# A hybrid encoder trunk on one core: the scan's first loads and first front move into the projections ahead of it, and filling products are left out in three places

## The chip, the core and the metric

One core of a Trainium2 chip. The metric is the device time of one execution in microseconds (us). Work runs on five engines with queues of their own: PE (TensorE, products; its weight loads are a row of their own, PEld), DVE (VectorE), ACT (ScalarE), POOL (GpSimd), and SP (SyncE), which here issues every DMA, in the order of its queue.

## The reference, cut to what matters

Two layers; each is a half-step FFN, a token mixer, a half-step FFN, with a layer norm after each. The first mixer is neighbourhood attention. The second, which is meant here, is a bidirectional RWKV-7 scan over 512 tokens, 16 heads of 64:

```python
xx = 0.5 * (x_prev + x_next) - x
xr, xw, xk, xv, xa, xg = (x + xx * mix[i] for i in range(6))
r, k, v = xr @ w_rkv[0], xk @ w_rkv[1], xv @ w_rkv[2]
wl = w0 + tanh(xw @ w1) @ w2                       # one per direction z
decay = exp(-exp(-softplus(-wl) - 0.5))
a = sigmoid(a0 + (xa @ a1) @ a2)
g = sigmoid(xg @ g1) @ g2
kk = normalised(k * k_k);  k_z = k * (1 + (a - 1) * k_a)
# per head, direction and token, with w, k_z, kk*a of that token:
sa = state @ (-kk)
state = state * w + outer(sa, kk * a) + outer(v, k_z);  y = state @ r
return (norm(y, forward + backward) + bonus(r, k_z, v)) * g @ w_out
```

## The kernel before, in words

Four FFNs, the attention and the scan follow each other. Weights are split by ACT and a second engine into a high and a low part, and a product is three products (`mm3`: lines 226, 227, 228).

**The projections** (`rwkv_project`) run in this order on PE, which keeps the order of the program text there: the keys (eight banks), the ranks `pw` and `pa`, the norm sums `ss` of the keys (L692), the receptances of the first pair of heads `pr` (L700; its inputs, the mixes `raws`, are computed by DVE at L648 into four `tmp` tiles in turn and stored as d_xr), the decays of direction 0 (`decays(0)`: 24 products, each evacuated by ACT and DVE and stored as d_lw), the gate's two ranks (L612), the decays of direction 1, and eight gate rows: six products each with the second gate weights `g2`, evacuated and stored as d_g. What the scan needs of all this it loads again from memory. Other engines and SP follow an order that a planner makes at build time from its own estimates: an instruction is placed when its inputs and its buffer are there, earlier text first.

**The scan** (`Scan`) treats pairs of heads, hp = 0 to 7. For each pair and direction `front` multiplies the decays with a triangle matrix (`tri`, L1234, cumulated decays), takes two exponentials, forms `a` (three products with `a2u` and `ah`) and builds the tiles `ar` and `bk`; `grams` (L1293) multiplies those; then come tails, values, an inversion on POOL, a chain over the chunks and the outputs. `load` fetches a pair's k, iv and a2. In the scan PE, ACT and DVE run in the order of lists (`SEQ`), one per slot n = -2 to 7. Ahead of slot -2, `run` loads ah, tri and the first pair, issues 33 filling products, and runs `front(0, 0)`; slot -2 begins with 17 more. Its list begins `g0 v f1 f1 f1 f1 f1 f1 g0 l g0 r r`: the first gram, the values' weights (`wv`), the second front, the next pair's `load`, and then `r`, steps of `receptances`. These are the receptances of pairs 1 to 7 (L1001, banks y and m); for them eight tiles of d_xr are loaded into az2, xs8 and xs9 and a weight of 512 KB at a time into other tiles of the scan, the first one after the eight.

A filling product (`busy`, L326) multiplies the identity by itself; nothing reads its result. It is there to keep PE at work while it would wait.

From slot 6 on, `outs` multiplies finished pairs with the output weights; the first five weights are loaded into the tiles wv, ar, ar, bk, bk.

The scan's tiles lie in two pools that open when the projections' pools have closed: `rwe` at the upper end of SBUF, over the weight pool, and `rwb` over everything else.

Of the kernel before, what the change touches and what calls it, by code (L numbers as in the profile page):

```python
# [10 lines left out]
F32 = mybir.dt.float32  # L11
# [79 lines left out]
def flat2(ap):  # L91
    return ap[:, :D], ap[:, D:]
# [6 lines left out]
class Trunk:  # L99
# [79 lines left out]
    def bank(self, tag="bank"):  # L179
        return self.ps.tile([P, 512], F32, name=tag, tag=tag, bufs=self.banks.get(tag))  # L180

# [397 lines left out]

    def rwkv_project(self, dram, xraw, w_rkv, w1, w2, a1, g1, g2, heads):  # L580

        nc = self.nc
        with self.pool("rwa") as pool:
            with self.behind(self.mid):
# [76 lines left out]
            with self.tc.manual_schedule(engines=MANUAL):  # L661
# [24 lines left out]
                low_rank(0, g1[:, :P], 5)  # L686
                g1b = pool.tile([P, ND, 32], F32, name="g1b")
# [9 lines left out]
                nc.sync.dma_start(dram["iv"], iv)  # L697
                pr = self.bank()
                for c, t in raws(0, dram["xr"]):
                    nc.tensor.matmul(pr, wr[:, c, :], t, start=c == 0, stop=c == ND - 1)  # L700
                with self.behind(self.lo, self.hi, self.mixed):
# [6 lines left out]
                def decays(z):  # L708
                    u = self.load_unit(w2[z])
                    for t in range(NT):  # L710
                        for h in range(2):
# [7 lines left out]
                            nc.sync.dma_start(dram["lw"][:, z, t, ws], th)  # L719
# [276 lines left out]
class Scan:  # L996
# [5 lines left out]

    def __init__(self, k, pool, dram, consts, a2, w_r, w_v, w_out):
        self.k, self.nc, self.pool, self.dram, self.a2, self.w_r, self.w_v, self.w_out = k, k.nc, pool, dram, a2, w_r, w_v, w_out
        nc = self.nc
        self.opened = ExitStack()
        early = self.early = self.opened.enter_context(k.pool("rwe", "right"))
        self.first = {}
        self.tri = early.tile([P, 2, P], F32, name="tri")
        self.mask = early.tile([P, 2, 2, CH], F32, name="mask")  # L1010
        self.onesb = early.tile([P, P], F32, name="onesb")
        self.eye = consts["eye"]
        self.ah = early.tile([P, 2, S], F32R, name="ah")
        self.xv = pool.tile([P, ND, S], F32, name="xv")
        self.consts = consts
# [12 lines left out]


        self.az = [(early if i == 2 else pool).tile([P, 2, NU, CH], F32, name=f"az{i}") for i in range(3)]  # L1030
        for i in range(2):
            self.clear(i)
        self.free = list(range(NBUF))
        self.taken, self.st, self.py = {}, {}, {}

# [3 lines left out]
    def tile(self, tag, shape, bufs=1, dtype=F32):  # L1039
        if tag in self.first:  # L1040
            return self.first.pop(tag)
        pool = self.early if tag in EARLY_TAGS else self.pool
        return pool.tile(shape, dtype, name=tag, tag=tag, bufs=bufs)
# [54 lines left out]
    def run(self, late, lead, ln):  # L1098
        with self.k.tc.manual_schedule(engines=MANUAL_SCAN):
            raw = self.tile("e", [P, S], 2)  # L1100
            for dst, src in ((raw, self.dram["ah"]), (self.tri, self.consts["tri"])):
                self.nc.sync.dma_start(dst, src)
            list(self.load(0))
            self.k.split(self.ah[:, 0, :], self.ah[:, 1, :], raw)
            self.k.busy(self.k.bank("c"), 33)
            list(self.front(0, 0))
            for n in ("mask", "onesb"):
                self.nc.sync.dma_start(getattr(self, n), self.consts[n])
            self.zs = []
# [12 lines left out]
            next(self.ending)  # L1122
# [59 lines left out]
    def slot(self, n):  # L1182
# [19 lines left out]
    def load(self, hp):  # L1202
# [11 lines left out]
        k.split(p.a2u[:, 0], p.a2u[:, 1], raw)  # L1214
        p.pc = tile_("pc", [P, NC, 2], 4)
        p.qd = tile_("qd", [P, NU, 32], 2)
        p.qc = tile_("qc", [P, NU, 32], 2)
        p.az = self.az[hp % 3]
        p.units, p.ar, p.bk = [], [], []
        yield  # L1220

    def front(self, hp, z):
# [7 lines left out]
        lw = tile_("lw", [P, NT, P], 2)  # L1230
        nc.sync.dma_start(lw, self.dram["lw"][:, z, :, hp * P : (hp + 1) * P])
        pi = k.bank("a")
# [11 lines left out]
        nc.scalar.activation(th, pa, AF.Tanh, scale=0.5, bias=k.col(C_A0H + z, hp))  # L1244
        ar = tile_("ar", [P, NC, 2, CH], 2)
        bk = tile_("bk", [P, NC, 2, CH], 2)
        at, rt = ar[:, way, 0, :], ar[:, way, 1, :]
# [14 lines left out]
        if z == 0:  # L1262
            nc.vector.scalar_tensor_tensor(p.iv, p.k, k.col(C_KKH, hp), p.iv, ALU.mult, ALU.mult)
        kz = tile_("kz", [P, S], 2)
        nc.scalar.activation(kz, th, AF.Identity, scale=k.col(C_KA1, hp), bias=k.col(C_KA2, hp))
# [219 lines left out]
    def outs(self):  # L1485
# [114 lines left out]
def trunk_kernel(tc, x, ffn_w_in, ffn_w_out, ln_g, ln_b, cols, w_qkv, b_qkv, bias, mask, w_o, b_o,  # L1600
                 w_rkv, w1, w2, a1, a2, g1, g2, rw_out, heads, tri, smask, onesb, eye, out):
    nc = tc.nc
    with ExitStack() as ctx:
# [12 lines left out]
        with k.activations(), k.psum(bank=8), k.weights(3):  # L1616
            k.load_x(grid(x))
            xT = k.new_xT()
            k.fill = {0: 11}
            for t in range(NT):  # L1620
# [8 lines left out]
            with ExitStack() as xs:  # L1629
                with k.behind(*k.last):  # L1630
                    xraw = k.ffn(xT, ffn_w_in[1, 0], ffn_w_out[1, 0], 3, lambda: XRaw(k, xs.enter_context(k.pool("xr"))))
                k.store_x(grid(dram["x"]))
                k.rwkv_project(dram, xraw.x, w_rkv, w1, w2, a1, g1, g2, heads)
        with ExitStack() as late:
            with k.pool("rwb") as pool:
                scan = Scan(k, pool, dram, dict(tri=tri, mask=smask, onesb=onesb, eye=eye), a2, w_rkv[0], w_rkv[2], rw_out)
# [79 lines left out]
```

## Time and profile before

| | |
|---|---|
| runs | 2238.38, 2242.78, 2242.82 us (median 2242.78) |
| the profiled execution | 2241.5 us, its span 2239.7 us |
| PE, DVE, ACT, POOL busy | 98%, 47%, 43%, 63% of the span |
| granted clock of PE, mean | 0.994 |
| DMA | 328.84 MB, mean 147 GB/s |
| filling products of the three places (L326, two passes each) | 22 passes from 1.37 us on; 66 from 1425.77 on; 34 from 1438.05 on |
| gate rows | 1411.5 to 1425.8 us |
| first receptance product of the scan | 1450.38 us |

How to read the profile: times are us from the start of the span. A row of the timeline has start, duration, engine, line, operation, the tiles out<-in, the count, and in brackets the engine's idle time before it with what ended it. In a window's row each engine has its busy time and, in brackets, its instructions; then come PE's granted clock (1.00 is full speed), the DMA engines' share, and GB/s. A row of the DMA issues has the tiles, the queue, the count, KB of each, and the median time from issue to landing. A busy PE is not a useful one: filling products count like all others.

### The profile page before, as it was taken

The numbers are of one execution on the slowest core, as the hardware profiler recorded it, in microseconds if no ns is written. First come the engines' busy times: TensorE is split into PE (matmuls) and PEld (weight loads), VectorE is DVE, ScalarE is ACT, GpSimd is POOL, SyncE is SP. The second block draws the span as 40 slices with busy tenths as digits, with TensorE's granted clock in tenths as the row PEclk, the third lists the DMA queues.
The fourth block names the chain that finished last, engine by engine and source line by source line (L and its number), as shares of the span: only waits on it lengthen the run. The fifth ranks groups of instructions, "written<-read, shape, count | busy, mean of one in ns | idle before, by whom it ended". The sixth has DMA issues, their size and how long they took to land. (4 is left out here: it accounts for less than half of the span.)

```text
span 2239.7 us, 35440 instructions
## 1 busy us (share of the span) xinstructions
PE 2187.5 (98%) x13972; PEld 1720.2 (77%) x13972; DVE 1063.5 (47%) x1524; ACT 957.6 (43%) x1678; POOL 1409.6 (63%) x1234
## 2 busy tenths in 40 slices
PE   8999999999999999999999999899999999999998
PEld 7888888887888888888888875535666657888886
DVE  2333356376433333643333587325788635333345
ACT  3333345377343333433333433336777633333333
POOL 6878855554487886588787442044776722888754
PEclk9999999999999999999999999999999999999999
DMA  6444463432344445454444545754454743544443
GB/s 199 143 143 147 145 230 97 131 93 84 110 141 144 145 143 170 135 184 141 142 137 140 197 131 191 231 158 126 114 141 111 207 151 99 160 142 136 141 169 122
DMA packets 350498, 328.84 MB, mean 147 GB/s; under 512 B 48458, under 2 KB 277450, under 8 KB 350332
## 3 DMA queue, kind: packets, MB, share of 16 engines
q1 hardware_dynamic: 350332, 326.58, 46.8%
q8 instruction: 110, 1.80, 0.3%
q14 instruction: 56, 0.46, 0.1%
HBM read 262.26 MB, written 47.74 MB: 138 GB/s over the span
## 5 line engine op out<-in xcount | busy, mean ns | idle before, releaser
L222 POOL TENSOR_TENSOR w<-raw,w 128x1024 fp32r<-128x1024 f32 x200 | 489.4, 2449 | 246.3 <-ACT w L221 222.7
L226 PE MATMUL bank<-xT,w 128*128 128x512 f32 x1408 | 549.3, 390 | 0.0
L227 PE MATMUL bank<-xT,w 128*128 128x512 f32 x1408 | 548.0, 389 | 0.0
L228 PE MATMUL bank<-xT,w 128*128 128x512 f32 x1408 | 547.9, 389 | 0.0
L221 ACT ACTIVATE w<-raw 128x1024 fp32r<-128x1024 f32 (+1 forms) x204 | 215.3, 1058 | 329.9 <-POOL ts L780 138.3
L428 DVE SCALAR_TENSOR_TENSOR ar<-bank,tmp 128x512 f32<-128x512 f32 x88 | 60.9, 692 | 578.3 <-PE bank L228 568.7
L228 PEld LDWEIGHTS bank<-xT,w 128*128 128x128 f32 x1408 | 264.3, 188 | 55.3
L227 PEld LDWEIGHTS bank<-xT,w 128*128 128x128 f32 x1408 | 264.4, 188 | 53.7
L226 PEld LDWEIGHTS bank<-xT,w 128*128 128x128 f32 x1408 | 264.4, 188 | 53.5
L809 PE MATMUL bank<-wx,an 128*128 128x512 f32 x792 | 187.3, 389 | 0.0
L1382 POOL TENSOR_TENSOR tm<-qs,zs 128x126 f32<-128x126 f32 (+22 forms) x248 | 106.0, 427 | 124.8 <-DVE qs L1375 74.7
L809 PEld LDWEIGHTS bank<-wx,an 128*128 128x128 f32 x792 | 148.7, 188 | 30.8
L809 PE MATMUL bank<-w,ring 128*128 128x512 f32 x720 | 168.8, 390 | 1.8 <-POOL w L222 1.7
L222 POOL TENSOR_TENSOR wx<-ra,wx 128x512 fp32r<-128x512 f32 x132 | 166.8, 1291 | 3.1 <-ACT wx L221 3.1
L222 DVE TENSOR_TENSOR ring<-ar,ring 128x1024 fp32r<-128x1024 f32 x44 | 131.8, 2996 | 73.3 <-ACT ring L221 73.3
L809 PEld LDWEIGHTS bank<-w,ring 128*128 128x128 f32 x720 | 134.9, 188 | 31.1 <-POOL w L222 2.8
L426 ACT ACTIVATE tmp<-bank 128x512 f32<-128x512 f32 x88 | 52.6, 597 | 223.8 <-PE bank L228 223.7
L222 POOL TENSOR_TENSOR ring<-raw,ring 128x1024 fp32r<-128x1024 f32 x28 | 68.4, 2451 | 96.3 <-ACT ring L221 96.3
L1384 POOL TENSOR_TENSOR zs<-zs,tm 128x126 f32<-128x126 f32 (+22 forms) x248 | 111.8, 451 | 19.4
L221 ACT ACTIVATE wx<-ra 128x512 fp32r<-128x512 f32 x132 | 82.9, 633 | 71.8 <-PE bank L809 67.9
L222 POOL TENSOR_TENSOR w<-late,w 128x1024 fp32r<-128x1024 f32 x30 | 76.0, 2538 | 59.7 <-ACT w L221 59.7
L226 PE MATMUL bank<-xT,ring 128*128 128x256 f32 (+1 forms) x352 | 102.3, 299 | 5.7 <-ACT ring L221 2.9
(275 smaller groups left out, 3777.5 us busy)
## 6 DMA issues: line engine op xcount, KB each, us to landing
raw<-in_ffn_w_in_dram SPq DMA_DIRECT2D x176, 512.0 KB, 3.9
ra<-in_ffn_w_out_dram SPq DMA_DIRECT2D x44, 1024.0 KB, 5.0
late<-d_late SPq DMA_DIRECT2D x34, 512.0 KB, 5.1
late<-in_ffn_w_out_dram SPq DMA_DIRECT2D x28, 512.0 KB, 4.4
raw<-in_w_qkv_dram SPq DMA_DIRECT2D x24, 512.0 KB, 4.1
d_late<-ts SPq DMA_DIRECT2D x44, 256.0 KB, 3.4
d_late<-ra SPq DMA_DIRECT2D x44, 256.0 KB, 2.0
xs<-ar SPq DMA_DIRECT2D x64, 128.0 KB, 2.4
```

What stands on the lines that cost most here:

```text
L221: self.hi = self.nc.scalar.activation(h, raw, AF.Copy).ins
L222: self.lo = (eng or self.nc.vector).tensor_tensor(l, raw, h.bitcast(F32), ALU.subtract).ins
L226: nc.tensor.matmul(out, wh, xh, start=start, stop=False)
L227: nc.tensor.matmul(out, wh, xl, start=False, stop=False)
L228: nc.tensor.matmul(out, wl, xh, start=False, stop=stop)
L426: nc.scalar.activation(s, pg, AF.Silu)
L428: nc.vector.scalar_tensor_tensor(raw[:, 3:7:3] if j else raw[:, 0:8:7], halves_of(pu), 0.5, halves_of(s), ALU.mult, ALU.mult)
L809: self.nc.tensor.matmul(acc, lhs, u[:, i], start=bool(first) and m == 0, stop=last and m == 2, skip_group_check=more)
L1382: nc.gpsimd.tensor_tensor(tv, qs[:, s, 0:s].rearrange("p (a o) -> p a o", o=1).broadcast_to([P, s, n]), zs[:, s : s + 1, c0:].broadcast_to ...
L1384: nc.gpsimd.tensor_tensor(zs[:, 0:s, c0:], zs[:, 0:s, c0:], tv, ALU.add)
```

## The change

- `Scan` is made in `rwkv_project`'s caller and handed in. The raw tokens `xraw` move to the upper end of SBUF; when the last mix is made they are closed, and `begin` opens a pool `rws` in their place: tri, mask, onesb, ah, the first pair's tiles, and both buffers of k, iv, r and lw for all pairs. `begin` loads ah, tri, the first pair, mask and onesb and splits ah.
- `fetch` loads the decays of the first pair, direction 0 after `decays(0)` and direction 1 after `decays(1)`.
- The first front's cumulated decays stand between `decays(1)` and the gate rows, and one further step of it after each gate row.
- The receptance products of the first pair come in two halves, four ahead of the norm sums `ss` and four after them.
- `run` starts with the slots. The 33 and the 17 filling products, and the 11 ahead of the very first transposes, are left out.
- `g1b` becomes a ring tile, and so do the tiles of the first front's exponentials. az2 moves to the scan's main pool. `ar`, `bk` and `kz` get one tile for each direction instead of two in turn. Two of the first output weights take the halves of az2 instead of one `ar` and one `bk` tile.

```diff
-EARLY_TAGS = ("k", "iv", "r", "lw", "kz", "a2r", "a2u", "v", "vr", "qc", "qd", "zs", "qs", "tm")
+START_TAGS = ("k", "iv", "r", "lw", "kz0", "ar0", "bk0", "a2r", "a2u", "pcs")
+EARLY_TAGS = ("kz1", "v", "vr", "qc", "qd", "zs", "qs", "tm")
...
+                pr, rs = self.bank(), raws(0, dram["xr"])
+
+                def receptance(n):
+                    for c, t in (next(rs) for _ in range(n)):
+                        nc.tensor.matmul(pr, wr[:, c, :], t, start=c == 0, stop=c == ND - 1)
+
+                receptance(ND // 2)
                 ss = self.bank()[:HEADS]
...
-                pr = self.bank()
-                for c, t in raws(0, dram["xr"]):
-                    nc.tensor.matmul(pr, wr[:, c, :], t, start=c == 0, stop=c == ND - 1)
+                receptance(ND // 2)
...
+                xs.close()
+                scan.begin()
                 decays(0)
+                scan.fetch(0, 0)
                 pg = [rank(0), rank(0, g1b)]
...
                 decays(1)
+                scan.fetch(0, 1)
+                start = scan.front(0, 0)
+                next(start)
                 ug = [self.load_rows(g2, 0), self.load_unit(g2[P:, :])]
                 for c in range(ND):
...
                     store(dram["g"][:, c, :], pp)
+                    next(start, None)
...
+    def begin(self):
+        nc = self.nc
+        pool = self.start = self.opened.enter_context(self.k.pool("rws", "right"))
...
+        ring = self.k.ring(F32)
+        raw, *rest = (ring[:, i * S : (i + 1) * S] for i in range(4))
+        self.first.update(zip(("e", "e2", "th"), rest))
+        for dst, src in ((raw, self.dram["ah"]), (self.tri, self.consts["tri"])):
+            nc.sync.dma_start(dst, src)
+        load = self.load(0)
+        next(load)
+        self.k.split(self.ah[:, 0, :], self.ah[:, 1, :], raw)
+        next(load)
+        for n in ("mask", "onesb"):
+            nc.sync.dma_start(getattr(self, n), self.consts[n])
...
     def run(self, late, lead, ln):
         with self.k.tc.manual_schedule(engines=MANUAL_SCAN):
-            raw = self.tile("e", [P, S], 2)
-            for dst, src in ((raw, self.dram["ah"]), (self.tri, self.consts["tri"])):
-                self.nc.sync.dma_start(dst, src)
-            list(self.load(0))
-            self.k.split(self.ah[:, 0, :], self.ah[:, 1, :], raw)
-            self.k.busy(self.k.bank("c"), 33)
-            list(self.front(0, 0))
-            for n in ("mask", "onesb"):
-                self.nc.sync.dma_start(getattr(self, n), self.consts[n])
...
-        if n == -2:
-            self.k.busy(self.k.bank("c"), 17)
...
+    def fetch(self, hp, z):
+        lw = self.lws[hp, z] = self.tile("lw", [P, NT, P], 2)
+        self.nc.sync.dma_start(lw, self.dram["lw"][:, z, :, hp * P : (hp + 1) * P])
...
-        w += [self.tile(n, [P, NC, 2, CH], 2).rearrange("p a b c -> p (a b c)") for n in ("ar", "ar", "bk", "bk")]
+        w += [self.az[2][:, i].rearrange("p a b -> p (a b)") for i in range(2)]
+        w += [self.tile(n, [P, NC, 2, CH]).rearrange("p a b c -> p (a b c)") for n in ("bk1", "ar1")]
...
-            k.fill = {0: 11}
...
-                k.rwkv_project(dram, xraw.x, w_rkv, w1, w2, a1, g1, g2, heads)
+                scan = Scan(k, dram, dict(tri=tri, mask=smask, onesb=onesb, eye=eye), a2, w_rkv[0], w_rkv[2], rw_out)
+                k.rwkv_project(dram, xraw.x, w_rkv, w1, w2, a1, g1, g2, heads, xs, scan)
```

More of the change, by code (lines that the diff above doesn't have):

```diff
@@ L179, in bank @@
     def bank(self, tag="bank"):
-        return self.ps.tile([P, 512], F32, name=tag, tag=tag, bufs=self.banks.get(tag))
+        tag = tag if tag in self.banks else "bank"
+        return self.ps.tile([P, 512], F32, name=tag, tag=tag, bufs=self.banks[tag])
     def load_unit(self, src, chunks=None, ring=False, eng=None):
@@ L577, in na_residual, with rwkv_project @@
             yield
-    def rwkv_project(self, dram, xraw, w_rkv, w1, w2, a1, g1, g2, heads):
+    def rwkv_project(self, dram, xraw, w_rkv, w1, w2, a1, g1, g2, heads, xs, scan):
         nc = self.nc
-        with self.pool("rwa") as pool:
+        if True:
             with self.behind(self.mid):
@@ L1001, in wide, with __init__, open @@
             self.nc.tensor.matmul(out[hs], w[:, hs], x, start=start, stop=stop)
-    def __init__(self, k, pool, dram, consts, a2, w_r, w_v, w_out):
-        self.k, self.nc, self.pool, self.dram, self.a2, self.w_r, self.w_v, self.w_out = k, k.nc, pool, dram, a2, w_r, w_v, w_out
-        nc = self.nc
[L1006 to L1013, printed above, removed]
+    def __init__(self, k, dram, consts, a2, w_r, w_v, w_out):
+        self.k, self.nc, self.dram, self.a2, self.w_r, self.w_v, self.w_out = k, k.nc, dram, a2, w_r, w_v, w_out
+        self.opened, self.consts = ExitStack(), consts
+        self.first, self.lws = {}, {}
+        self.free = list(range(NBUF))
+        self.taken, self.st, self.py = {}, {}, {}
+    def begin(self):
+        nc = self.nc
+        pool = self.start = self.opened.enter_context(self.k.pool("rws", "right"))
+        self.tri = pool.tile([P, 2, P], F32, name="tri")
+        self.mask = pool.tile([P, 2, 2, CH], F32, name="mask")
+        self.onesb = pool.tile([P, P], F32, name="onesb")
+        self.ah = pool.tile([P, 2, S], F32R, name="ah")
+        ring = self.k.ring(F32)
[9 more added lines that the diff above has]
+            nc.sync.dma_start(getattr(self, n), self.consts[n])
+    def open(self, pool):
+        self.pool = pool
+        early = self.early = self.opened.enter_context(self.k.pool("rwe", "right"))
+        self.eye = self.consts["eye"]
         self.xv = pool.tile([P, ND, S], F32, name="xv")
-        self.consts = consts
         unit = lambda i: (pool.tile([P, 2, 4, 2, CH], F32, name=f"xs{i}"), pool.tile([P, 2, 4, CH], F32, name=f"tb{i}"))
@@ L1027, in __init__ @@
         self.units = [units[i] for i in range(NBUF)]
-        self.az = [(early if i == 2 else pool).tile([P, 2, NU, CH], F32, name=f"az{i}") for i in range(3)]
+        self.az = [pool.tile([P, 2, NU, CH], F32, name=f"az{i}") for i in range(3)]
         for i in range(2):
             self.clear(i)
-        self.free = list(range(NBUF))
-        self.taken, self.st, self.py = {}, {}, {}
+        self.room(0)
     def place(self, tag, shape, bufs=1):
@@ L1041, in tile @@
             return self.first.pop(tag)
-        pool = self.early if tag in EARLY_TAGS else self.pool
+        pool = self.start if tag in START_TAGS else self.early if tag in EARLY_TAGS else self.pool
         return pool.tile(shape, dtype, name=tag, tag=tag, bufs=bufs)
@@ L1630, in trunk_kernel @@
                 with k.behind(*k.last):
[L1631 removed]
+                    xraw = k.ffn(xT, ffn_w_in[1, 0], ffn_w_out[1, 0], 3, lambda: XRaw(k, xs.enter_context(k.pool("xr", "right"))))
                 k.store_x(grid(dram["x"]))
[L1633 removed]
+                scan = Scan(k, dram, dict(tri=tri, mask=smask, onesb=onesb, eye=eye), a2, w_rkv[0], w_rkv[2], rw_out)
+                k.rwkv_project(dram, xraw.x, w_rkv, w1, w2, a1, g1, g2, heads, xs, scan)
         with ExitStack() as late:
             with k.pool("rwb") as pool:
[L1636 removed]
+                scan.open(pool)
                 with k.psum(a=2, g=2, p=1, c=1, m=1, y=1):
```

26 lines of the change are left out of this document (15 added, 11 removed).

## The prediction

> **What bounds the kernel now.** I read the page first, then windows around the place that the change touches, then the timeline there, then the DMA issues of the same stretch.
>
> ```profile
> span 2239.7 us, 35440 instructions
> PE 2187.5 (98%) x13972; PEld 1720.2 (77%) x13972; DVE 1063.5 (47%) x1524; ACT 957.6 (43%) x1678; POOL 1409.6 (63%) x1234
> ```
>
> TensorE is busy 98% of the span, so a change can win only where PE waits, or where what PE does is not needed. The second case is easy to miss: filling products count as busy. The windows, in order: two ranks of the gate projection, the gate rows, the stretch from the last gate product to the first gram, the rest up to the first receptance product, and what follows (columns: busy time and instructions by engine, granted clock, DMA share, GB/s).
>
> ```profile
> core 0: us, PE busy (x) PEld busy (x) DVE busy (x) ACT busy (x) POOL busy (x), PEclk, DMA share, GB/s
> 1395.00:1405.00 10.00, 10.00 (x25) 3.10 (x24) 1.12 (x2) 1.23 (x2) 1.16 (x1) 1.00 0.00 0
> 1411.50:1425.80 14.30, 14.30 (x50) 7.62 (x48) 0.85 (x2) 4.92 (x9) 2.07 (x4) 1.00 0.54 205
> 1425.80:1443.10 17.30, 14.86 (x112) 14.18 (x111) 6.03 (x10) 4.54 (x9) 0.00 (x0) 0.90 0.98 299
> 1443.10:1450.40 7.30, 2.98 (x29) 2.38 (x29) 4.72 (x8) 4.64 (x12) 0.00 (x0) 0.94 0.99 316
> 1450.40:1458.00 7.60, 7.60 (x32) 2.66 (x32) 0.82 (x2) 0.00 (x0) 0.00 (x0) 0.61 1.09 305
> ```
>
> DMA does nothing from 1395 to 1405, half its time in the gate rows, and is then full at 299 to 316 GB/s until the receptance products begin. The timeline says what PE's 14.86 us were:
>
> ```profile
> 1425.77 7.63 PE L326 MATMUL c<-ident 128*128 128x128 f32 x66
> 1435.37 1.61 PE L1234 MATMUL a<-tri,lw 128*128 128x128 f32 x8 [1.97 <-DMA lw<-d_lw]
> 1438.05 4.57 PE L326 MATMUL c<-ident 128*128 128x128 f32 x34
> 1443.11 1.16 PE L1293 MATMUL g<-ar,bk 64*128 64x128 f32 x16 [0.48 <-DVE bk L1271]
> 1444.20 1.16 PE L1234 MATMUL a<-tri,lw 128*128 128x128 f32 x8
> 1445.11 0.48 PE L226 MATMUL a<-ah,a2u 128*128 128x512 f32 x1
> 1445.66 0.40 PE L228 MATMUL a<-ah,a2u 128*128 128x512 f32 x1
> 1450.38 6.62 PE L1001 MATMUL y<-az,xs 128*64 128x512 f32 x16 [4.32 <-DMA xs<-in_w_rkv_dram]
> ```
>
> 12.2 us are filling products, 7.63 and 4.57. What ends this stretch is the last line: the first receptance product waits for its weights. So from 1425.8 to 1450.4, 24.6 us, the bound is the stream of loads, and the fronts, grams and filling products lie beside it. That the gram at 1443.11 waited for the first front's last DVE result (L1271) is a wait inside a wait.
>
> **The change part by part.** *Loads moved out of that stream.* The issues from 1426 to 1450 (KB each, us to landing), and the one row of the stretch before that belongs to them:
>
> ```profile
> DMA packets 6938, 7.26 MB, mean 303 GB/s; under 512 B 489, under 2 KB 4457, under 8 KB 6937
> iv<-d_iv SPq DMA_DIRECT2D x4, 128.0 KB, 4.4
> lw<-d_lw SPq DMA_DIRECT2D x2, 256.0 KB, 7.1
> a2r<-in_a_dram SPq DMA_DIRECT2D x2, 128.0 KB, 4.7
> e<-d_ah SPq DMA_DIRECT2D x1, 256.0 KB, 4.2
> r<-d_r SPq DMA_DIRECT2D x1, 256.0 KB
> k<-d_k SPq DMA_DIRECT2D x1, 256.0 KB
> mask<-in_smask_dram SPq DMA_DIRECT2D x1, 128.0 KB, 5.4
> onesb<-in_onesb_dram SPq DMA_DIRECT2D x1, 64.0 KB, 5.0
> tri<-in_tri_dram SPq DMA_DIRECT2D x1, 128.0 KB
> ```
>
> Half of iv and of a2r, and the k shown, are the second pair's; the first pair's k, also 256 KB, went out just before 1426. Moved by the text of the change: tri 128, k 256, iv 256, a2r 128, ah 256 (the row e), r 256, both lw 512, mask 128, onesb 64: 1,984 KB, 2.03 MB, at 303 GB/s 6.7 us. They go into stretches where DMA has room: 10 us at a share of 0.00 and 46% of 14.3 us. On SP they now stand among the stores of the decays and of the gate: a fetch of lw waits there for the stores that it reads, and what is queued behind it are the second pass's stores or the gate's. PE waits for those only through the evacuation buffers, eight in turn, so a microsecond or two there costs nothing; what PE waits for directly is a rival below.
>
> The second pair's k, iv and a2r (256 + 256 + 128 = 640 KB, 0.66 MB, 2.2 us) stay in the scan's program. But in the changed kernel their tiles stand in a pool that is already open during the projections, and the order on SP's queue is the planner's, which issues a load when its buffer is free:
>
> ```profile
> 1369.33 0.59 SPq L190 DMA_DIRECT2D raw<-in_g_dram x1
> 1411.53 0.40 PE L226 MATMUL bank<-ring,w 128*128 128x512 f32 x1
> ```
>
> The gate's second weights were asked for 42 us ahead of the rows that use them, and ahead of the decays written before them. So I take these 2.2 us as gained too; the other end is 0. The stream is shorter by 8.9 us, or by 6.7.
>
> *PE work moved into the projections.* The first front's products now stand between PE's own instructions: from 1444.20 to 1445.66, the second front's at full clock, is 1.46 us for all but the last product, and that one takes as long as each of the two before it, 0.28 (half of 1445.11 to 1445.66): 1.7 us. The gate rows end that much later, and with them the buffers of the loads that remain. So the first receptance product comes 8.9 - 1.7 = 7.2 us earlier, or 5.0.
>
> *What covers the moved front.* Its DVE and ACT steps take 6.03 and 4.54 us in the window 1425.8 to 1443.1, and the gate rows leave DVE 13.4 and ACT 9.4 us idle: nothing. Without that cover the gram would wait, inside the same 13 us of idle PE. The second front runs in that idle time; from L1234 at 1444.20 it took until
>
> ```profile
> 1450.56 0.69 DVE L1271 SCALAR_TENSOR_TENSOR bk<-th,e 128x512 f32<-128x512 f32 x1
> ```
>
> 7 us, less than the 15.7 us that now pass between the last gate row (1427.5) and the receptances (1443.2). Late next is the same load as before.
>
> *Filling products left out.* The 12.2 us are waits by another name: 0. What they could have done is keep the clock up, but the window from 1450.4 has a granted clock of 0.61 after an idle time of only 4.32 us: at half speed for 5.9 of its 7.6 us, 3.0 us lost. The window from 1425.8 (0.90 of 17.3 us) gives 3.5 us at half speed, 1.7 lost. A longer idle time ends in the same cold start: 0, with 1.2 us to either side. At the kernel's start (the third place):
>
> ```profile
> 13.11 1.09 PE L334 MATMUL bank<-ident,x 128*128 128x128 f32 x8 [1.09 <-DMA x<-in_x_dram]
> 15.97 0.58 PE L226 MATMUL bank<-xT,ring 128*128 128x256 f32 x1 [1.76 <-ACT ring L221]
> ```
>
> The transposes wait for x, and the first product after them for a weight's split, not for them: 0. Slowed to half, the last four transposes would end 1.1 us later, at 15.3, still ahead of 15.97; ends 0 and 1.1. [...]
>
> *Receptance products of the first pair in two halves.*
>
> ```profile
> 1370.01 7.04 PE L692 MATMUL bank<-ring,heads 128*16 128x512 f32 x16
> 1376.98 3.70 PE L700 MATMUL bank<-tmp,wr 128*128 128x512 f32 x8
> 1382.97 3.70 PE L700 MATMUL bank<-tmp,wr 128*128 128x512 f32 x8 [2.29 <-DVE tmp L648]
> 1373.66 0.74 DVE L648 SCALAR_TENSOR_TENSOR tmp<-ring,cols,xraw 128x512 f32<-128x512 f32 x1
> 1374.98 0.74 DVE L648 SCALAR_TENSOR_TENSOR tmp<-ring,cols,xraw 128x512 f32<-128x512 f32 x1
> ```
>
> The first four products now come at 1370.0, each 0.88 (7.04 / 8). If DVE still delivers the third and fourth tile at 1374.4 and 1375.7, PE waits 2.6 and 0.4 us there, 0.8 more than the 2.29 that go; if DVE brings them forward, 2.3 are won. I take 0, nearer to DVE's order as it stands; ends +0.8 and -2.3.
>
> *Output weights in other tiles.* Two of the scan's first output weights move from ar and bk tiles into the halves of az2, which the outputs of pair 5 read last:
>
> ```profile
> 1778.51 0.45 PE L1474 MATMUL y<-vt,az 64*64 64x64 f32 x8
> 1784.79 1.08 PE L1001 MATMUL a<-ar,xv 128*64 128x512 f32 x4
> DMA to landing us min/median/max: 6.4/7.3/8.3
> ```
>
> (The third row is that of L1506, the same kind of load.) Issued at 1779.0, such a weight lands at 1785.4 to 1787.3, for a use at 1784.8: 0.6 to 2.5 us late, on PE's path. I take 1.0; ends 0 and 2.5.
>
> *Sum:* -7.2 + 0 + 0 + 0 + 1.0 = **-6.2 us**. The profiled execution took 2241.5, its span 2239.7 and 1.8 around it; it lies between the runs shown (2238.38 to 2242.82, median 2242.78). Forecast: 2241.5 - 6.2 = **2235.3**.
>
> **The rivals.** *A load that PE's fixed order now waits for (slower).* The first front's cumulated decays stand right ahead of the gate rows. Their input lw must be stored and fetched again, and SP works in order through
>
> ```profile
> 1388.49 25.43 SPq L719 DMA_DIRECT2D d_lw<-ring x16
> ```
>
> If the fetch stands behind all 16 stores, it goes out at 1413.9 and lands, at 7.1 us, at 1421.0: PE waits 9.5 us at 1411.5, and everything behind is late by that much. The idle time would bring the cold start, 3.0 more. 2235.3 + 12.5 = 2247.8. It decides from a landing later than 1411.5 + 6.2 = 1417.7. For it: PE's order is written by hand, and SP's stores are issued as DVE delivers them. Against: the first pass's stores are done before the window 1395 to 1405, in which DMA moves nothing and the planner has room for the fetch.
>
> *The gain is given back in small parts (no change).* Second pair not early (5.0 instead of 7.2), receptances +0.8, output weights +2.5, so a gain of 1.7: 2239.8. For it: each part stands in a row above. Against: all three must fall on the bad side.
>
> *A larger gain.* If DVE brings the tiles forward (2.3) and the remaining stream flows at the 316 GB/s of the second window instead of 303 (the 24.6 us less 8.9 are 15.7; 4% of them 0.6), 2232.4; with a shorter cold start (1.2), 2231.2. [...]
>
> **How the numbers follow.** Forecast 0.50, larger gain 0.12, no change 0.22, slower 0.16. A measurement tells about 0.2% from no change, 4.5 us; the first two cases lie beyond it: faster 0.62, same 0.22, slower 0.16. Range: the good ends give 2241.5 - 7.2 - 2.3 - 1.2 = 2230.8, the bad ones 2241.5 - 5.0 + 0.8 + 2.5 + 1.1 + 1.2 = 2242.1; rounded out to 2230 and 2243 it leaves out most of the slower rival, and a little of the larger gain.
>
> **What would show it.** Right: loads at DMA in the idle stretch before 1405; no filling product between the gate rows and the receptances; the first gram directly after the last gate row, at about 1427.5; the first receptance product at about 1443, still waiting for its weights, PE idle some 13 us before it and cold after it. Wrong: a wait for lw or tri at L1234 in the projections; k, iv and a2r of the second pair among the loads after the last gate row (then 5.0); more than 2.3 us of wait in the receptance products; more than 2.5 us at the first output products. If the receptances come 7 us earlier and the time does not move, a later wait has taken the gain.

## The result, and the profile after

| | before | changed |
|---|---|---|
| runs, median (lowest to highest) | 2243.22 us (2237.72 to 2245.82), 12 runs | 2243.85 us (2241.85 to 2250.08), 12 runs |
| the profiled execution | 2241.5 us, span 2239.7 | 2242.69 us, span 2240.9 |

The ratio is 1.001, with a 95% interval from 1.0 to 1.0019: no difference that counts, where 2235.3 had been forecast. The moved work went where it was meant to go, though. First lines of the page of the changed kernel, then the timeline of PE from the last gate rows on:

```profile
span 2240.9 us, 35205 instructions
...
PE 2175.0 (97%) x13850; PEld 1706.6 (76%) x13850; DVE 1060.0 (47%) x1524; ACT 958.0 (43%) x1678; POOL 1411.7 (63%) x1234
```

```profile
1412.09 1.05 PE L1266 MATMUL bank<-tri,lw 128*128 128x128 f32 x8
...
1427.90 1.16 PE L1324 MATMUL g<-ar,bk 64*128 64x128 f32 x16
1429.00 1.16 PE L1266 MATMUL a<-tri,lw 128*128 128x128 f32 x8
...
1447.02 5.94 PE L1015 MATMUL y<-az,xs 128*64 128x512 f32 x16 [16.16 <-DMA xs<-in_w_rkv_dram]
```

PE is busy for 12.5 us less, and the span is 1.2 us longer. The first front's cumulated decays (1412.09) wait for nothing, the first gram comes directly after the last gate row, at 1427.90 instead of 1443.11, and the first receptance product comes at 1447.02 instead of 1450.38. Setting the two traces product by product against each other shows where the time went (changed minus before, in us; each figure is the difference of two starts):

| place | difference |
|---|---|
| first FFN's products, at 43 us | +1.2 |
| last rank ahead of the first pair's receptances, at 1370 | +1.8 |
| after the first pair's receptances | +0.6 |
| first receptance product of the scan | -3.35 |
| after its sixteen products | -4.05 |
| up to the output products (1745) | -5.3 |
| first output product with az2 (1785) | +0.5 |
| behind the first output products with az2 (1790) | +2.4 |
| from 1820 on, and end of PE | +1.2 |

So three places are to be explained: +1.2 at the start, a gain of 4 instead of 7 at the receptances, and 5.8 lost at the output products, with 1.9 more right behind. The 0.6 between 43 and 1370 us are small waits; this stretch takes from 1326.5 (e7) to 1330.2 us (e3) in the thirteen traces of this case. Here is the start (timeline of PE in the changed kernel; then the first of the FFN's products at full speed, in the kernel before and in the changed one):

```profile
6.43 4.06 PE L336 MATMUL bank<-ident,x 128*128 128x128 f32 x16 [6.43 <-DMA x<-in_x_dram]
10.76 1.97 PE L336 MATMUL bank<-ident,x 128*128 128x128 f32 x8 [0.27 <-DMA x<-in_x_dram]
12.97 1.90 PE L336 MATMUL bank<-ident,x 128*128 128x128 f32 x8 [0.24 <-DMA x<-in_x_dram]
```

```profile
22.83 0.28 PE L227 MATMUL bank<-xT,ring 128*128 128x256 f32 x1
25.00 0.28 PE L228 MATMUL bank<-xT,ring 128*128 128x256 f32 x1
```

Eight transposes take 1.9 to 2.0 us instead of 1.09. They end only 0.7 later, but the products of the first FFN take 0.41 each from 19.3 to 24.65, at a granted clock of 0.50, and 0.28 from 25.0 on (from 22.8 in the kernel before); the 1.2 us are lost there. The first product behind them, of the next matrix, comes at 44.19 instead of 42.98. Whether the missing filling products are the reason is looked at under e1.

The receptances' loads, by SP's timeline, the waits of SP, and the DMA issues of 1427 to 1447:

```profile
1399.95 0.44 SPq L1229 DMA_DIRECT2D k<-d_k  x1
1400.43 1.12 SPq L1231 DMA_DIRECT2D iv<-d_iv  x2
1401.65 0.58 SPq L1233 DMA_DIRECT2D a2r<-in_a_dram  x1
...
1429.01 0.42 SPq L1356 DMA_DIRECT2D wv<-in_w_rkv_dram  x1
1429.53 0.71 SPq L1090 DMA_DIRECT2D az<-d_xr  x1
1430.34 1.35 SPq L1336 DMA_DIRECT2D az<-xs  x2
1431.74 1.57 SPq L1090 DMA_DIRECT2D az<-d_xr  x3
1436.62 1.13 SPq L1337 DMA_DIRECT2D xs<-ar  x2
1437.79 2.23 SPq L1090 DMA_DIRECT2D xs<-d_xr  x4
1440.07 0.43 SPq L1095 DMA_DIRECT2D xs<-in_w_rkv_dram  x1
```

```profile
SPq L1337 <- DMA az<-xs: 3.2, 1, 3.2
```

```profile
DMA packets 4878, 5.28 MB, mean 264 GB/s; under 512 B 832, under 2 KB 2880, under 8 KB 4877
...
az<-xs SPq DMA_DIRECT2D x2, 64.0 KB, 6.2
```

The second pair's k, iv and a2r went out at 1400, as forecast. The grams' own small transfers (az<-xs, xs<-ar) are new here: the first gram is done 15 us earlier, so SP takes them up between the loads of the receptances' inputs, and the second of them waits 3.2 us for the landing of the first, with four inputs and the weight queued behind it. The 512 KB of wv go out ahead of all of them, as they did before. In the kernel before, the first grams' transfers went out at 1450.41, behind the weight. The mean rate is 264 GB/s, not the 303 of before.

Last the output weights: PE's first products with az2 (timeline), SP's issues, and the landing by the DMA issues of 1765 to 1790.

```profile
1785.28 1.98 PE L1015 MATMUL a<-az,xv 128*64 128x512 f32 x4 [5.68 <-DMA az<-in_rw_out_dram]
```

```profile
1772.45 0.54 SPq L1527 DMA_DIRECT2D bk<-in_rw_out_dram  x1
1773.08 0.40 SPq L1527 DMA_DIRECT2D wv<-in_rw_out_dram  x1
1773.53 0.42 SPq L1538 DMA_DIRECT2D xs<-in_rw_out_dram  x1
1774.33 0.33 SPq L1536 DMA_DIRECT2D ar<-in_rw_out_dram  x1
1774.71 0.61 SPq L1538 DMA_DIRECT2D xs<-in_rw_out_dram  x1
...
1775.84 0.44 SPq L1527 DMA_DIRECT2D az<-in_rw_out_dram  x1
...
1776.86 0.60 SPq L1527 DMA_DIRECT2D az<-in_rw_out_dram  x1
```

```profile
az<-in_rw_out_dram SPq DMA_DIRECT2D x2, 512.0 KB, 9.8
```

The two weights that are used second and third are issued last of seven, 3,584 KB within 4.4 us, and land 9.8 us after their issue. PE waits 5.7 us, and the products behind this wait begin at half speed (a granted clock of 0.50 from 1785.28 to 1787.3): the first four take 1.98 us instead of 1.08, and 1.9 us more are lost by 1790. In the kernel before, the first of the ar and bk tiles had taken their weights long ahead:

```profile
1763.09 0.46 SPq L1495 DMA_DIRECT2D ar<-in_rw_out_dram  x1
...
1769.80 0.38 SPq L1495 DMA_DIRECT2D bk<-in_rw_out_dram  x1
```

At 1820 the changed kernel gets 1.3 us back. There PE idles in the middle of 64 small products, with nothing that the profile names as the reason ("issue"), by the waits of PE before and after:

```profile
PE p L1422 <- issue: 2.1, 1, 2.1
PE p L1453 <- issue: 0.8, 1, 0.8
```

The traces of e2, e3, e5, e7 and e9 have this idle time too (0.7 to 1.3 us), those of e1, e4, e6, e8, e10 and e11 do not. Of the filling products that the kernels differ in, these six have the ones ahead of the first transposes and no others. So in the thirteen traces this idle time goes with which filling products a kernel has; why was not tested.

### The profile page after: what moved, and what is told of

Same layout as the page of the kernel before. It is cut to its first block, busy times and chain, and to the rows that moved or that the text cites. A ratio compares the mean times of both kernels' runs of the same rounds, so it can differ in the third digit from the quotient of the medians.

```text
span 2240.9 us, 35205 instructions
## 1 busy us (share of the span) xinstructions
PE 2175.0 (97%) x13850; PEld 1706.6 (76%) x13850; DVE 1060.0 (47%) x1524; ACT 958.0 (43%) x1678; POOL 1411.7 (63%) x1234
```

## The experiments

The first three edits are each aimed at one of the three losses in the changed kernel; one profiled execution each.

**e1: the eleven filling passes ahead of the first transposes put back.**

```diff
             xT = k.new_xT()
+            k.fill = {0: 11}
             for t in range(NT):
```

> The changed kernel with the 11 filling products ahead of the first transposes put back. Theory (the missing fill leaves PE at half speed from its first transpose on): the transposes take 1.09 us for eight again instead of 1.97, the FFN's products reach full speed about 1.6 us earlier, and every product after them stands 1.6 us earlier than in the changed kernel (norm sums of the keys at 1375.0 instead of 1376.6 us). [...]

2243.98 us. In this execution only the first sixteen transposes are at full speed (1.09 us for eight; the next two groups of eight take 1.97 and 1.66), yet the first product of the next matrix is 1.85 us earlier than in the changed kernel (42.34), and 1.0 us is left of it at 1370. Behind that, waits for weights take it back (az2's is 4.2 here), and the end is 1.3 later. The traces of the other kernels settle what this single one can't (us, by the starts and durations of products):

| kernels | filling products ahead of the transposes | FFN's products at full speed from | first product of the next matrix |
|---|---|---|---|
| before | yes | 22.8 | 42.98 |
| changed | no | 25.0 | 44.19 |
| e2, e3, e5 | no | 22.6, 22.6, 22.9 | 43.53, 42.97, 43.16 |
| e1, e4 | yes | 21.3, 22.7 | 42.34, 42.96 |
| e6 to e11 | yes | 22.8 to 24.3 | 43.05 to 43.76 |

Of the kernels without the filling products, e3 is as early as the kernel before and e5 0.2 us later, and three of the kernels with them (e6, e7, e8) are later than both. The means at 43 us are 43.46 without and 43.16 with them. So what differed by 1.2 us between the two profiled executions is the point at which the clock rises, and that point differs by 2.4 us among the four traces without the filling products and by 3.0 among the nine with them. That the filling products move it at all is not shown; by the means it is 0.3 us.

**e2: the output weights in an order in which the az2 halves are used sixth and seventh.**

```diff
-        w += [self.az[2][:, i].rearrange("p a b -> p (a b)") for i in range(2)]
+        xs = [self.units[i][0].rearrange("p a b c d -> p (a b c d)") for i in (2, 4, 3)]
+        w += xs[:2]
         w += [self.tile(n, [P, NC, 2, CH]).rearrange("p a b c -> p (a b c)") for n in ("bk1", "ar1")]
-        w += [self.units[i][0].rearrange("p a b c d -> p (a b c d)") for i in (2, 4, 3)]
+        w += [self.az[2][:, i].rearrange("p a b -> p (a b)") for i in range(2)] + xs[2:]
```

> The changed kernel with the output weights in another order of the same tiles: the second and third weight in two xs tiles, the halves of az2 last, for weights that are used only behind the scan. Theory (the 5.68 us of wait at the output products come from az2, which is read until the end of slot 5, so that its weights are issued last and land behind 2.5 MB of others): the wait falls to 0 to 1.5 us, and the products of slot 6 stand 4 to 5.7 us earlier against the changed kernel. Rival (seven weights in one burst are late whatever their tiles, because the burst is bound by bandwidth): the wait stays at 4 to 6 us, on another tile.

2238.35 us. By SP's timeline of this kernel the az2 halves are still issued last:

```profile
1772.81 0.54 SPq L1528 DMA_DIRECT2D xs<-in_rw_out_dram  x1
1773.44 0.40 SPq L1528 DMA_DIRECT2D wv<-in_rw_out_dram  x1
...
1775.94 0.44 SPq L1539 DMA_DIRECT2D az<-in_rw_out_dram  x1
...
1776.99 0.77 SPq L1539 DMA_DIRECT2D az<-in_rw_out_dram  x1
```

But PE no longer waits there (the product after the first weight's comes at 1781.94 with no idle time). Against the changed kernel the difference goes from +0.7 at 1775 to -4.4 behind these products: 5.1 us. The wait of 5.7 is gone. The four products at this place take 1.97 us, as cold as in the changed kernel (1.98), and the next four 1.08 instead of 1.42; the products just ahead of the place are slower here (the first with wv takes 1.11 us instead of 0.64).

**e3: the receptances' first loads ahead of the grams' transfers, in the program text.**

```diff
             if hp == 1:
+                yield
                 for c in range(ND):
                     nc.sync.dma_start(self.xv[:, c, :], self.dram["xv"][:, c, :])
...
             self.zs = []
+            self.rs, self.out = self.receptances(), self.outs()
+            next(self.rs)
             for _ in range(2):
                 self.unit()
-            self.rs, self.out = self.receptances(), self.outs()
```

> The changed kernel with the eight loads of d_xr and the first receptance weight written ahead of slot -2, so that on SP they stand ahead of the values' weights and of the first gram's transfers az<-xs and xs<-ar. Theory (SP waited 3.2 us for az<-xs to land, and 1.1 us more to issue xs<-ar, with half of d_xr and the weight queued behind; and 512 KB of wv went first): the first receptance product comes 5 to 8 us earlier than 1447.0, at 1439 to 1442. Rival (the stream is bound by bandwidth from the last gate row on, and the order on SP does not matter): 1446 to 1447, or 1445 by the 512 KB of wv alone.

2239.81 us. SP's timeline of this kernel:

```profile
1430.42 1.88 SPq L1090 DMA_DIRECT2D az<-d_xr  x4
1432.35 2.38 SPq L1090 DMA_DIRECT2D xs<-d_xr  x4
1436.05 0.38 SPq L1095 DMA_DIRECT2D xs<-in_w_rkv_dram  x1
1436.69 0.56 SPq L1358 DMA_DIRECT2D wv<-in_w_rkv_dram  x1
1437.41 3.93 SPq L1338 DMA_DIRECT2D az<-xs  x2
```

The weight is issued at 1436.05 instead of 1440.07, PE's wait falls from 16.2 to 10.4 us, and the product comes at 1442.60 although the path ahead of it is 1.4 later: 5.8 us won at this place. That is about the 3.2 us of wait and 2.5 us of issues that stood ahead of the weight. The edit also takes the 512 KB of wv from ahead of these loads; that these bytes have no part in the 5.8 us was not tested alone. The weight itself lands 6.5 us after its issue, 6.8 in the changed kernel. The end is 2.9 earlier.

**e4: all three edits.**

> The three edits together: fill ahead of the first transposes, loads of the receptances first on SP, output weights with az2 last. Theory (three separate waits on PE's path, which add): 1.6 + 5 to 8 + 4 to 5.7 us below the changed kernel, so 2228 to 2233 us, 0.5% to 0.7% below the kernel before. Rival (what is won at the scan's start is lost in a later wait of the scan, on POOL's inversion or on loads): less than 5 us below the kernel before.

2231.03 us (2228.91 to 2235.6), before on the same chip 2240.12; ratio 0.9954 (0.9937 to 0.9971), five rounds. It beats both kernels. The first receptance product stands at 1440.02, 10.4 us earlier than before, and PE's last instruction comes 12.5 earlier. (2.3 of these 12.5 are the idle time at 1820, which this kernel doesn't have.)

**e5: the first pair's receptances in one piece behind `ss`, the rest as changed.**

> The changed kernel with the first pair's eight receptance products in one piece behind the norm sums, as in the kernel before. Theory (the two halves win 1.0 us: DVE's third and fourth tile cost 0.7 us of wait ahead of the norm sums, and the 2.29 us of wait behind them go): the products of the decays stand 1.0 us later than in the changed kernel, with a wait of 2.3 us for tmp in the second four. Rival (the halves win nothing, the 1.0 us are DVE's order elsewhere): within 0.3 us.

2240.61 us. Against the changed kernel the difference is -1.39 us ahead of the place and -1.33 behind it: the two halves win 0.06. PE's timeline of this kernel shows why:

```profile
1377.43 3.70 PE L696 MATMUL bank<-tmp,wr 128*128 128x512 f32 x8
1382.22 3.70 PE L696 MATMUL bank<-tmp,wr 128*128 128x512 f32 x8 [1.09 <-DVE tmp L650]
```

In one piece the wait for DVE is 1.09 us (2.29 before the change); in two halves it is 0.52 and 0.20. The 1.2 us that the changed kernel wins at this place against the kernel before (from +1.8 to +0.6) are there in one piece too.

**e6 and e11: the kernel before, without the scan's 33 and 17 filling passes.** One profiled execution, then five rounds.

```diff
-            self.k.busy(self.k.bank("c"), 33)
...
-        if n == -2:
-            self.k.busy(self.k.bank("c"), 17)
```

> The kernel before without the 33 and the 17 filling products ahead of the scan, nothing else. Theory (they lie wholly inside waits for loads, and the clock is cold at the receptances with or without them): the first receptance product stays at 1450.4 us, within 0.7, the granted clock from there on at 0.6 for 7.6 us as before, and the end of the kernel unchanged. Rival (they kept the clock up for the first front and gram, whose products then lie on the path): the receptances 1 to 3 us later.

> The kernel before without the scan's two places of filling products (33 and 17), timed in rounds this time; the start's filling products stay. Theory (the filling products ended too early to keep the clock for the receptances, while the front's and the gram's own products, slowed, do; leaving them out wins 2.5 to 4 us behind 1450): 2 to 4 us faster than the kernel before. Rival (the single time of this edit lay within the spread of the kernel before): within 1 us of it.

2238.24 us, a single time within the spread of the kernel before on that chip (2237.2 to 2245.3), then 2237.91 us (2233.15 to 2241.05), before 2239.53; ratio 0.9986 (0.9975 to 0.9996): 1 to 6 us faster, 3 by the ratio and 1.6 by the medians. Timeline of PE in e6, and its windows of the same stretches as in the prediction:

```profile
1444.36 2.08 PE L1290 MATMUL g<-ar,bk 64*128 64x128 f32 x16 [4.84 <-DVE bk L1268]
1446.37 2.07 PE L1231 MATMUL a<-tri,lw 128*128 128x128 f32 x8
...
1450.38 3.65 PE L1001 MATMUL y<-az,xs 128*64 128x512 f32 x16 [0.65 <-DMA xs<-in_w_rkv_dram]
```

```profile
1425.80:1443.10 17.30, 4.16 (x14) 2.87 (x14) 4.86 (x9) 4.54 (x9) 0.52 (x2) 0.70 0.95 293
1443.10:1450.40 7.30, 5.39 (x29) 4.34 (x29) 3.75 (x7) 1.73 (x3) 0.00 (x0) 0.53 1.02 346
1450.40:1458.00 7.60, 7.60 (x48) 3.00 (x49) 4.25 (x7) 3.95 (x13) 0.00 (x0) 1.00 1.11 334
```

The first receptance product starts at the same 1450.38, but sixteen take 3.65 us instead of 6.62. Without filling, the gram and the second front run at half clock (0.53 over 1443.1 to 1450.4), inside the wait for the weight; that spreads them over the time up to 1450, and the clock is full when the receptances begin (1.00 over 1450.4 to 1458). With filling they ran at full clock (1.00 over 1443.1 to 1446.1) and were done at 1446; the clock was 0.91 over the idle 4.2 us from 1446.1 to 1450.3, and 0.50 over 1450.4 to 1456, under the receptances. In e11's profiled execution, of the same program, the sixteen take

```profile
1449.98 5.18 PE L1001 MATMUL y<-az,xs 128*64 128x512 f32 x16 [1.32 <-DMA xs<-in_w_rkv_dram]
```

so how much is won here differs from one execution to the next (3.65 and 5.18 us for the same sixteen products of one program): behind the sixteen products e6 is 3.0 us ahead of the kernel before, e11 1.8. The lead is not simply carried to the end, though. At the output products both lose 4 us again, and e11 is 1.3 behind the kernel before at 1815; its trace then wins 2.3 at the idle time of 2.1 us in L1422, which e6 and e11 don't have. So the 3 us of the ratio are measured, and how they divide between the warmer clock and that idle time is open.

**e7: e4 with 44 filling passes right ahead of the first receptance product.**

```diff
             pr = self.k.bank("ym"[i % 2])
+            if i == 0:
+                self.k.busy(pr, 44)
             for c in range(ND):
```

> The kernel with the three edits (fill, loads first, output weights) and 44 filling products right ahead of the first receptance product, 10.2 us of a wait of 10.8 us. Theory (a product that begins after more than 4 us of idle PE runs at half clock for about 6 us, which costs 3 us): the first receptance products take 3.65 us for sixteen instead of 5.9, and what follows stands 2 to 3 us earlier than in the kernel with the three edits. Rival (the weights land earlier than the fill ends, or the clock does not matter since the later loads set the pace): 0 to 1 us, either way.

2233.64 us (2232.97 to 2236.53), before 2241.12; ratio 0.9966 (0.9954 to 0.9979). PE's timeline of this kernel:

```profile
1429.00 9.99 PE L328 MATMUL y<-ident 128*128 128x128 f32 x88
1440.47 3.65 PE L1015 MATMUL y<-az,xs 128*64 128x512 f32 x16 [1.48 <-DMA xs<-in_w_rkv_dram]
```

The sixteen take 3.65 us instead of 6.57 in e4, and PE is 2.5 us ahead behind them. By 1653 only 0.6 of that is left, and at the output products it is lost with more, since the planner now puts wv behind four other output weights (the waits of PE):

```profile
PE a L1015 <- DMA wv<-in_rw_out_dram: 4.2, 1, 4.2
```

Another 3.2 us go in the middle of the 64 small products of L1457, at 1811, where PE idles 1.3 us, and behind it; e4 has no idle time there.

**e8: e4 with the two loads of `zs` queued behind the first receptance weight.**

> The kernel with the three edits, and the two zs loads (512 KB, for the inversion, which comes much later) queued on SP behind the first receptance weight. Theory (what ends the wait is the number of bytes ahead of the weight; 0.52 MB at 303 GB/s): the first receptance product comes 1.7 us earlier than 1440.0, at 1438.3. Rival (zs is issued before the last gate row and lands while SP would wait for the pool to close): less than 0.5 us earlier.

2229.83 us (2229.46 to 2230.14), before 2241.12; ratio 0.9948 (0.9934 to 0.9961). The first receptance product comes at 1439.93, against 1440.02 in e4, with a path ahead of it that is 0.9 later: about 0.9 us is won at this place, and the ratio's interval overlaps that of e4. SP issues the weight 1.2 us earlier than in e4 (1431.98 instead of 1433.16), but it lands after 7.9 us instead of 6.8: with the queue out of the way, an earlier issue no longer brings the weight as much earlier.

**e9: e7 with wv issued first of the output weights.**

```diff
-            nc.sync.dma_start(w[i], rows(self.w_out, i))
+            with self.k.behind(*([wv.ins] if i else [])):
+                ld = nc.sync.dma_start(w[i], rows(self.w_out, i))
+            wv = ld if i == 0 else wv
```

> The three edits with 44 filling products ahead of the first receptance product, and in the last slot the first output weight (wv) issued ahead of the other output weights, as it is with the three edits alone. Theory (the warm clock wins 2.5 us at the receptances, and the kernel with fills lost it again only because wv went out behind the other output weights): no output product waits 4 us for wv, the receptances take 3.65 us, the total is 2 to 3 us under the kernel with the three edits, about 2228. Rival (what is won at the receptances is given back by the loads after them in any case, since DMA is full there): the first receptances take 3.65 us again, and the total stays within 1 us of the three edits alone, 2230 to 2232.

2231.38 us (2229.36 to 2232.23), before 2239.51; ratio 0.9961 (0.9947 to 0.9975). The wait for wv is down to 0.5 us, and PE is 2.6 us ahead of e4 behind the receptances. At 1653 0.55 of it is left, at 1800 1.5. Then 3.0 us are lost within 6 us, as in e7: PE idles 1.2 us in L1457, and the eight output products behind take 3.7 us instead of 2.1. PE's end is 2.5 later than in e4's profiled execution, and the ratios overlap. So with the filling products the receptances do run warm (a granted clock of 1.00 over 1440.3 to 1444, against 0.55 over 1440.0 to 1446.6 in e4), and here most of what was lost later stands at this idle time, which e4 doesn't have. That without it the warm clock would show in the total was not tested.

**e10: e1 and e2 together, the loads as the change left them.**

> The changed kernel with two of the three edits: the start's filling products, and the output weights in the order that gives the halves of az2 to the last of them. The scan's loads stay as the change left them. Theory (the change's gain at the receptances is real and carried, and was lost at two other places, 1.6 us at the start and 5.7 us at the output weights): 2243.9 less 5 to 7 us, about 2237.5, with the first receptance product still at about 1445.5 and its wait still 16 us; the remaining 6 us of the kernel with all three edits belong to the order of the loads. Rival (the output weights are only where a lateness that arises elsewhere shows itself, and the time comes back in other waits): within 2 us of the changed kernel.

2236.95 us (2234.46 to 2241.02), before 2239.53; ratio 0.9986 (0.9976 to 0.9996), 0.0024 under the changed kernel, 5.4 us of 2240. The first receptance product comes at 1445.51 and still waits 15.4 us. At the az2 place the difference against the changed kernel goes from -2.1 at 1775 to -7.2 behind it: 5.1 us, as in e2; another 1.05 is the idle time at 1820, which e10 doesn't have. What is left between e10 and e4, 0.0032 or 7.2 us (5.5 by their spans), is the order of the loads, the only edit in which they differ.

## Why the prediction was wrong, point by point

- **Loads moved out of the stream** (8.9 less 1.7, first receptance product 7.2 us earlier): the loads moved, the second pair's too, and the first gram is 0.4 from its forecast. The product came 3.35 earlier, with a path ahead of it 0.6 late: 3.9 won at this place. The step that failed is the sentence "late next is the same load as before": the stream was taken as a sum of bytes at one rate, and the order of SP's queue in it as given. The gram's earlier end put a dependent pair of small transfers ahead of the weight, with a wait of 3.2 us and 2.5 us of issues. With the loads in front (e3) it takes 5.8 us less, and in e4 the product is 10.4 earlier than before. That speaks for the 7.2 as what the moved bytes allow; it isn't shown, as these edits also put the 512 KB of wv behind the weight.
- **Output weights** (1.0; ends 0 and 2.5): 5.7 of wait and 1.9 of products at half speed behind it; 5.4 in the timed runs of e10, which also has the start's filling products. This is the second step that failed. The term was mis-sized twice. The landing, 6.4 to 7.3 us by the rows of before, was 9.8 behind five other weights in one burst. And the issue was counted from the last read of az2 alone, while a scan that is 5.3 us ahead needs its weights 5.3 us earlier: they went out 2 to 3 us earlier than was assumed. The bound of 2.5 came from a row whose surroundings the change had changed.
- **Start without filling** (0; ends 0 and 1.1): 1.2 in the profiled executions, 0.3 by the means of all traces, so 0 was near the truth. The transposes did run at about half speed (eight take 1.97 us instead of 1.09), as its upper end had it, and end 0.7 later (1.1 there). What the forecast didn't look at are the FFN's products behind them, which reach full speed at 25.0 instead of 22.8 in this execution and at 22.6 to 22.9 in three others without filling.
- **Filling products in the scan** (0; 1.2 to either side): in the kernel before, leaving them out is worth 1 to 6 us (e11). One way is seen in e6: with the front and the gram done late and slow, PE idles 0.65 us ahead of the receptances instead of 4.3, and the clock over 1450.4 to 1458 is 1.00 instead of 0.61. In the changed kernel the front no longer lies in this wait, PE idles 16 us, and the sixteen products are cold again, 5.94 us. So at this place 0 was near the truth for the change, and the reason given for it too. The forecast did not see that leaving them out of the kernel before is worth about half of what was forecast for the whole change, nor that the idle time at 1820 changes with them (from 2.1 to 0.8 us).
- **Halves of the first receptances** (0): right. The wait of 2.29 fell to 0.72, but it falls to 1.09 without the halves (e5).
- **The rivals.** The slower one, PE waiting for lw at the gate rows, did not occur: lw went out at 1402.33, in the idle stretch. "Given back in small parts" comes nearest: it named the output weights, at 2.5 where they took 5.7. The forecast's own last sentence holds: the receptances came earlier, the time did not move, and a later wait had taken the gain.

The parts give the measured +1.2 of the profiled executions: +1.2 at the start and +0.6 up to 1370, -5.85 from the first pair's receptances through the scan's first receptances (from +1.8 to -4.05), -1.3 up to 1745, +7.8 at the output weights and the cold products behind, and -1.3 at 1820. The losses at the loads' order and at the output weights were each removed by their own edit, and both by e4; the start's was gone in traces without any edit to it. Of the 8.6 us between the forecast and the median of the changed kernel, 1.7 lie in the value that the forecast started from: the profiled execution, 2241.5, was faster than the median of the twelve runs of before, 2243.22.

## What to carry to other kernels

When a step moves forward, list what becomes free with it: everything that waited for it may now be issued into the queue that was to be relieved, ahead of the transfer that sets the end. Cost a load by the burst that it is issued in and by its time of use on the new schedule, not by its landing in the old one: here 9.8 us where 6.4 to 7.3 had been read. And ask of filling products when they end. In the kernel before, 12.2 us of them were followed by the gram, the second front and 4.3 us of idle PE, and the sixteen products took 6.62 us; in e7, 10 us of them ended 1.5 us ahead, and the sixteen took 3.65. Before an edit is given a microsecond, compare all traces that have it with all that lack it: the clock's rise at the start came anywhere from 22.6 to 25.0 us in the four traces without filling products there.

## What the hardware showed that was not expected

- The granted clock's column reads 1.00 over the first 16.5 us of the changed kernel, while its transposes take nearly twice their time (1.97 us for eight, 1.09 in the kernel before). The duration of a known instruction was the better witness here. The row of the windows:

```profile
0.00:16.50 16.50, 7.78 (x33) 6.28 (x33) 5.99 (x13) 7.04 (x11) 0.74 (x7) 1.00 0.92 217
```

- A pair of transfers of 64 KB from tile to tile took 6.2 us to land in the full stream of the scan's start (the queue at 91% of the DMA engines from 1427 to 1447; 2.5 us at 50%, e7 from 1752 to 1762), nearly as long as the weight of 512 KB behind it (6.8).
- A cold start costs the sixteen products 1.5 to 3.0 us, and the cost differs between executions: 5.18 to 6.62 us in the ten traces where they start cold, 3.65 in the three where they start warm (e6, e7, e9).
- PE idled 0.7 to 2.1 us in the middle of 64 equal small products without a wait that the profile names, in the same group of products in seven kernels and not at all in six; the two sets differ in their filling products.
